# A two-layer attention and feed-forward trunk: places of the first loads, order of the context products, and four edits further on

## The chip, the cores and the metric

The kernel runs on one core of one Trainium2 chip. The metric is the time of one execution on the device in microseconds (us); the median of several runs is given. A core has a matrix engine (TensorE, PE in the profile), VectorE (DVE), ScalarE (ACT), GpSimd (POOL) and SyncE (SP), each with an instruction queue of its own, and DMA engines that move data between device memory and the on-chip memory.

## The reference

512 latent tokens and 256 context tokens of width 1024 go through two layers. Layer 0 has differential attention (4 heads) and neighbourhood attention (8 heads) side by side, layer 1 has windowed grouped-query attention with sink logits (16 query heads on 4 key heads, window 128). Every layer ends in a SwiGLU feed-forward network (FFN) of 2816 hidden columns.

```python
def rmsnorm(x, g):
    y = xf * lax.rsqrt(jnp.mean(xf * xf, axis=-1, keepdims=True) + NORM_EPS)
    return y * g
def modulate(h, shift, scale):
    return h * (1 + scale) + shift
def swiglu(h, w1, w3, w2):
    return (jax.nn.silu(h @ w1) * (h @ w3)) @ w2
# in each layer, for latent and for context tokens:
#   six modulation vectors from silu(c) @ ada_w + ada_b
#   x = x + gate_1 * mixer(modulate(rmsnorm(x, norm_g), shift_1, scale_1))
#   x = x + gate_2 * swiglu(modulate(rmsnorm(x, norm_g), shift_2, scale_2))
# after both layers: out = rmsnorm(x, final_g), latent tokens only
```

Latent queries read the latent keys and all context keys in one softmax; queries and keys of the latent tokens are rotated by position (rotary embedding). Context tokens read context tokens only, and leave after layer 0 except for their keys and values in layer 1.

## The kernel before, in words

All activations lie transposed, 128 of the 1024 features on the partitions (chunks k = 0 to 7), tokens along the columns. Each matrix product is made of three on TensorE, with both operands split into a high and a low part: high x high, high x low, low x high (`mm3`, lines 209 to 211 and their like). Weights come from device memory as `raw` tiles of 512 KB; ACT rounds the high part, DVE subtracts for the low one (`split`, lines 198 and 199; `split_by_dma`, lines 203 to 205, lets a DMA that adds do the subtraction). The class `Stream` S loads weights in the order of their use through SP's queue into a pool with three places and splits them ahead.

The order of work is set in two ways. Under `manual_schedule` an engine does its instructions in the order of the code: the start up to the first attention, for all five engines, and the second attention and the start of the second FFN for four. Elsewhere the Tile scheduler orders the instructions of each engine by itself, from the order in which the code issues them.

**Start.** `ada_load(b, k)` brings the modulation weights (b = 0, 1, eight chunks each), `w_load` four projection weights (keys, queries, two of values: `wk_raw`, `wq_raw`, `wv0_raw`, `wv1_raw`). Four modulation weights share the pool `wpool` (tag "raw") with the projection weights; TensorE reads the modulation weights at line 237. Then come the latent products (line 786), and the context part: sums of squares (`c_sq`, lines 853 to 857), their norm (lines 901 to 911), the chunks of modulated context `c_t` and `c_lo` (lines 918 to 923), and the context's products (lines 937 to 939). `rope_read` and `rope_end` (lines 891 to 896) rotate keys (`psk`) and queries (`psq`) from PSUM; `evac_pair` writes keys and queries, `swap_halves` makes `k2`, the keys with halves exchanged, through two DMAs; `v_group` is the context's values.

**First attention.** Eight units of heads, each with five steps; `run_steps` issues a step's scores (lines 1055 and 1056 for the differential heads) and softmax, then the value products of the step before, then some filling work `fillers[n]`, mostly the next unit's queries, keys and values.

**First FFN.** Products go by the `seven` products of a scheme for 2 x 2 blocks. In its last part (`down_last` at line 1583, products at lines 1563 to 1565) eight chunks m of latent and then eight of context columns get their residual on DVE (line 1557), and in the second of these loops `next_norm` makes the second layer's first norm: squares on ACT, additions on DVE and GpSimd (lines 331 to 340), a product with ones that sums over partitions (line 308), logarithm and exponential on ACT (lines 315 to 318), and `h_make` (lines 352 to 354). `apart=True` leaves three sums to be added by three products with ones.

**Second attention.** A loop over n = 0 to 33 in set order: scores (line 1748), the masked maximum on DVE (`masked`, line 1758), exponentials on ACT (`powers`, line 1765), value products four steps later; `fill(counts[n][0])` and `fill(counts[n][1])` place that many filling products before and behind the transposes, the output projection's among them (lines 1882 and 1906, residual line 1867). `to_make` queues weight roundings (lines 1828 and 1829).

**Output.** The second FFN's own `down_last` makes the last four chunks' products of the second FFN for two halves of 256 tokens, `final_norm` the norm of a half, `put_out` multiplies eight pieces on DVE and GpSimd (line 2278) and stores each (line 2279).

## Time and profile before

| What | us |
|---|---|
| Median of 3 runs | 1590.34 (1589.73 to 1591.67) |
| The profiled execution | 1589.07 |
| Its span from first to last instruction | 1587.3 |
| TensorE busy | 1544.8 |
| DVE, ACT, GpSimd busy | 1225.2, 729.7, 265.0 |

The page has busy times first, then the span in 40 slices, DMA queues, the chain of work that ended last, and groups of instructions. A row of the timeline begins with start and duration; "L308" is line 308; "f<-norm,ones" is output and inputs by the program's names; in brackets stands the idle time of the engine ahead of the row and whom it waited for. Matmuls overlap in a pipeline, so the distance of their starts is what one costs. "SPq" is SP's instruction queue. In windows, each engine has its busy us and instructions, then the granted clock of TensorE (1.00 is full), the share of the DMA engines, and GB/s.

### The profile page before, as it was taken

What the parts mean: (1) busy time and instruction counts of PE and PEld (TensorE: products, weight loads), DVE (VectorE), ACT (ScalarE), POOL (GpSimd) and SP (SyncE); (2) the same over time, 40 slices, a digit from 0 to 9 for tenths busy, and PEclk for the clock granted to TensorE, in tenths of its full rate; (3) what the DMA queues carried; (4) which work ended last, traced back from release to release, by engine and by line L of the source; (5) the groups of instructions that cost most, each with busy time, mean ns of one, the idle gap of its engine ahead of it and who ended that gap; (6) DMA issues with size and microseconds to landing.
All of it is one profiled execution on the core that took longest, in us unless ns stands there. A gap on an engine that the chain in (4) does not pass through costs nothing.

```text
span 1587.3 us, 25721 instructions
## 1 busy us (share of the span) xinstructions
PE 1544.8 (97%) x10029; PEld 1372.5 (86%) x10029; DVE 1225.2 (77%) x2090; ACT 729.7 (46%) x1242; POOL 265.0 (17%) x340
## 2 busy tenths in 40 slices
PE   8999999999999999999999999999999999999997
PEld 5898988877878999989999997877768899989896
DVE  4767798966698789879798867677666887869686
ACT  4555554445354423424424254366655533425254
POOL 1032223462010000000100002255320000000001
PEclk9999999999999999999999999999999999999999
DMA  9422254543236465475766653311013442422321
GB/s 333 127 66 74 77 176 128 185 137 93 70 120 165 115 181 159 140 210 162 215 177 166 206 135 99 92 42 41 28 54 79 134 146 80 134 67 94 121 79 54
DMA packets 68897, 196.93 MB, mean 124 GB/s; under 512 B 6836, under 2 KB 19284, under 8 KB 68776
## 3 DMA queue, kind: packets, MB, share of 16 engines
q1 hardware_dynamic: 58136, 159.95, 32.0%
q0 software_dynamic: 9632, 34.03, 9.8%
q8 instruction: 79, 1.29, 0.3%
q10 hardware_dynamic: 1008, 1.31, 0.2%
q14 instruction: 42, 0.34, 0.1%
HBM read 161.04 MB, written 4.86 MB: 105 GB/s over the span
## 4 chain that ended last, share of the span: by engine, by line
PE 57%; DMA 4%; issue 3%; DVE 3%; ACT 1%; DVEq 0%; SPq 0%; ACTq 0%; POOLq 0%; POOL 0%
PE f L1524 5%; PE f L1522 5%; PE f L1523 5%; PE f L2197 4%; PE f L2199 4%; PE f L2198 4%; PE f L1563 3%; PE f L1564 3%; PE f L1565 3%; PE lin L1859 2%; PE f L2251 2%; PE f L2250 2%; PE f L2252 2%; PE s L1748 2%; PE t L410 2%
## 5 line engine op out<-in xcount | busy, mean ns | idle before, releaser
L198 ACT ACTIVATE wh<-raw 128x1024 fp32r<-128x1024 f32 (+1 forms) x96 | 92.1, 977 | 235.6 <-DVE raw L539 94.5
L199 DVE TENSOR_TENSOR wl<-raw,wh 128x1024 fp32r<-128x1024 f32 (+1 forms) x96 | 106.9, 1119 | 40.6 <-ACT wh L198 39.1
L209 PE MATMUL lin<-hb,wh 128*128 128x512 f32 (+1 forms) x352 | 121.9, 347 | 4.1 <-ACT hb L1295 2.4
L210 PE MATMUL lin<-hb,wh 128*128 128x512 f32 (+1 forms) x352 | 119.9, 341 | 0.5 <-DVE hb L1296 0.5
L211 PE MATMUL lin<-hb,wl 128*128 128x512 f32 (+1 forms) x352 | 119.6, 340 | 0.0
L271 DVE SCALAR_TENSOR_TENSOR junk<-raw,tables 128x1024 bf16<-128x1024 f32 x80 | 98.6, 1233 | 15.6 <-DMA raw<-in_ada_wT_dram 15.1
L204 POOL DMA_DIRECT2D wl<-raw x39 | 34.1, 874 | 444.2 <-ACT wl L203 417.5
L1563 PE MATMUL f<-g,wh 128*128 128x512 f32 (+1 forms) x304 | 102.7, 339 | 0.2 <-DVE s L1552 0.2
L1564 PE MATMUL f<-g,wh 128*128 128x512 f32 (+1 forms) x304 | 102.7, 339 | 0.0
L2198 PE MATMUL f<-hb,wh 128*128 128x256 f32 x360 | 101.6, 283 | 0.0
L2197 PE MATMUL f<-hb,wh 128*128 128x256 f32 x360 | 101.4, 283 | 0.0
L2199 PE MATMUL f<-hb,wl 128*128 128x256 f32 x360 | 101.2, 283 | 0.0
L1565 PE MATMUL f<-g,wl 128*128 128x256 f32 (+1 forms) x304 | 100.7, 336 | 0.0
L1522 PE MATMUL f<-hb,wh 128*128 128x384 f32 x288 | 96.2, 334 | 0.0
L1523 PE MATMUL f<-hb,wh 128*128 128x384 f32 x288 | 96.2, 334 | 0.0
L1524 PE MATMUL f<-hb,wl 128*128 128x384 f32 x288 | 96.2, 334 | 0.0
L209 PEld LDWEIGHTS lin<-hb,wh 128*128 128x128 f32 x352 | 66.6, 189 | 15.0 <-ACT hb L1295 2.9
L210 PEld LDWEIGHTS lin<-hb,wh 128*128 128x128 f32 x352 | 66.7, 189 | 8.3 <-DVE hb L1296 0.7
L338 POOL TENSOR_TENSOR ns_a<-ns_a,ns_s 128x256 f32<-128x256 f32 (+1 forms) x8 | 8.4, 1054 | 388.3 <-ACT ns_s L334 388.3
L211 PEld LDWEIGHTS lin<-hb,wl 128*128 128x128 f32 x352 | 66.6, 189 | 7.1
L1524 PE MATMUL f<-T,wl 128*128 128x384 f32 x216 | 72.2, 335 | 0.4 <-DVE wl L199 0.4
L1522 PE MATMUL f<-T,wh 128*128 128x384 f32 x216 | 72.2, 334 | 0.0
(521 smaller groups left out, 4918.7 us busy)
## 6 DMA issues: line engine op xcount, KB each, us to landing
raw<-in_w_dram SPq DMA_DIRECT2D x132, 512.0 KB, 3.8
raw<-in_ada_wT_dram SPq DMA_DIRECT2D x80, 512.0 KB, 3.8
wl<-raw POOLq DMA_DIRECT2D x41, 512.0 KB, 6.2
raw<-in_w_ab_dram SPq DMA_DIRECT2D x24, 512.0 KB, 4.1
raw<-in_ada_w_dram SPq DMA_DIRECT2D x12, 512.0 KB, 7.7
raw<-in_w_c_dram SPq DMA_DIRECT2D x12, 512.0 KB, 4.0
nb<-in_na_bias_dram POOLq DMA_DIRECT2D x16, 256.0 KB, 3.2
raw<-in_wo_ab_dram SPq DMA_DIRECT2D x8, 512.0 KB, 3.7
```

The source lines that it names most:

```text
L209: nc.tensor.matmul(ps, wh(k), xh(k), start=k == 0, stop=False)
L210: nc.tensor.matmul(ps, wh(k), xl(k), start=False, stop=False)
L211: end = nc.tensor.matmul(ps, wl(k), xh(k), start=False, stop=k == n - 1)
L1522: nc.tensor.matmul(ps, wh(k), b[:, 0, :], start=k == 0, stop=False)
L1523: nc.tensor.matmul(ps, wh(k), b[:, 1, :], start=False, stop=False)
L1524: nc.tensor.matmul(ps, wl(k), b[:, 0, :], start=False, stop=k == 3)
L1563: nc.tensor.matmul(ps, hi, g[:, 0, cols[v]], start=first, stop=False)
L1564: nc.tensor.matmul(ps, hi, g[:, 1, cols[v]], start=False, stop=False)
L1565: nc.tensor.matmul(ps, lo, g[:, 0, cols[v]], start=False, stop=last)
L2197: nc.tensor.matmul(ps, wh(k), b[:, 0, :], start=k == 0, stop=False)
L2198: nc.tensor.matmul(ps, wh(k), b[:, 1, :], start=False, stop=False)
L2199: nc.tensor.matmul(ps, wl(k), b[:, 0, :], start=False, stop=k == 3)
```

## The change

It has five parts. (1) Four more of the modulation weights' chunks get places in buffers of the attention that are free at the start; none takes a place in `wpool` any more. (2) In the context part both `rope_read` move behind the chunks of context, one copy of values ahead of them; the context's keys and queries get other PSUM tiles; the fillers of the first step run ahead of the steps. (3) At the first FFN's end one more pair of weights is split by ACT and DVE, `next_norm` runs at m = 2 instead of 4 with one product with ones instead of three, and the activation table is loaded behind a copy. (4) In the second attention some filling products move by a step, and the last roundings are queued for the step behind the last scores. (5) The output part is written in set order, with one product with ones for the first half and two for the second, multiplications of 512 columns on DVE alone, and eight stores of 256 KB instead of sixteen of 128 KB.

```diff
@@ -559,7 +559,7 @@
...
         t = tpool[0]().rearrange("p a b n -> p (a b n)")
         hi, lo = t[:, 0:1024], t[:, 1024:2048]
-        (split if i == 1 else split_by_dma)(hi, lo, raw[0])
+        (split if i in (1, 3) else split_by_dma)(hi, lo, raw[0])
@@ -686,14 +686,17 @@
...
-            ada_at = {(1, 5): wide[1][:, NX : 3 * NX], (1, 6): sp.tile([P, 2 * NT + 128], F32, tag="q", name="xs")[:, 0:1024]}
+            ada_at = {(1, 5): wide[1][:, NX : 3 * NX]}
+            for key, tag, n in (
+                ((1, 6), "q", 2 * NT + 128), ((0, 5), "q", 2 * NT + 128), ((0, 6), "k1", 2 * NT), ((0, 7), "v", 2 * NT), ((1, 7), "k2", 2 * NT),
+            ):
+                ada_at[key] = sp.tile([P, n], F32, tag=tag, name="xs", bufs=1 if tag == "k2" else 2)[:, 0:1024]
...
-                    z = wpool if (b, k) in ((0, 5), (0, 6), (0, 7), (1, 7)) else pa
-                    t = z.tile([P, 1024], F32, tag="raw" if z is wpool else "ada", name="raw")
+                    t = pa.tile([P, 1024], F32, tag="ada", name="raw")
@@ -904,7 +907,6 @@
...
             rus = [rp.tile([P, NX], F32, tag="ru", name="ru", bufs=1), p0.tile([P, NX], F32, tag="ns_s", name="ru", bufs=2)]
-            rope_read(0, psk)
@@ -924,30 +926,35 @@
...
+            vunits[0] = sp.tile([P, 6, 256], F32, tag="v", name="v")
+
+            def v_copy(t):
+                nc.scalar.copy(vunits[0][:, 2 + 2 * t : 4 + 2 * t, :], psv[t][:, :, 0:256])
+
+            v_copy(0)
             c_t(0)
-            rope_read(1, psq)
             for k in range(KT):
                 if k < KT - 1:
                     c_t(k + 1)
                 c_lo(k)
-            pck, pcq = linp(), linp()
+            v_copy(1)
+            rope_read(0, psk)
+            rope_end(0)
+            pck, pcq = tp(), tp()
...
-            vunits[0] = sp.tile([P, 6, 256], F32, tag="v", name="v")
-            for t in range(2):
-                nc.scalar.copy(vunits[0][:, 2 + 2 * t : 4 + 2 * t, :], psv[t][:, :, 0:256])
-            rope_end(0)
             evac_pair(units[0]["k"], NC, NX, ropes[0], 1.0)
             evac_pair(units[0]["k"], 0, NC, pck[:, 0:NC], 1.0)
             swap_halves(units[0]["k2"], units[0]["k"])
+            rope_read(1, psq)
...
-            ps = tp().rearrange("p (t c) -> p t c", t=2)
+            ps = sp2((P, 2, 512))[:, :, 0:256]
             v_group(ps, 0, [tuple(wslice(z, 256) for z in w[0:2]) for w in (wv0, wv1)])
@@ -1351,7 +1358,9 @@
...
             fillers += spread(fl, len(us))
-        run_steps(steps, fillers)
+        for f in fillers[0]:
+            f()
+        run_steps(steps, [[]] + fillers[1:])
@@ -1438,7 +1447,9 @@
...
             pool = Carve([half(z, i) for z in t for i in range(2)])
-            r = rstd_of(fps(), sq_sum(xr, pool, apart=True), D, pool)
+            a, b = sq_sum(xr, pool)
+            nc.vector.tensor_add(a, a, b)
+            r = rstd_of(fps(), [a], D, pool)
             for k in range(KT):
@@ -1597,7 +1608,7 @@
...
-                if m == 4:
+                if m == 2:
                     next_norm()
@@ -1619,9 +1630,7 @@
...
-                    act = nc.scalar.activation(q, q, AF.Silu)
-                    if p == HT // 2 - 1:
-                        exp_ln_tables(act)
+                    nc.scalar.activation(q, q, AF.Silu)
                     rows(1 if p > 2 else 0, end)
@@ -1632,6 +1641,8 @@
...
                     g_made[:] = [nc.scalar.copy(g[:, 0, :], q), nc.vector.tensor_sub(g[:, 1, :], q, f32(g[:, 0, :]))]
+                    if p == HT // 2 - 1:
+                        exp_ln_tables(g_made[0])
@@ -1888,7 +1899,7 @@
...
                         keys = k2.rearrange("p a b n -> p (a b n)")
                         to_make([keys[:, 0:1024], keys[:, 1024:2048]], last)
-                        to_make()
+                        to_make(ready=last + 1)
@@ -1928,7 +1939,7 @@
...
-            (0, 4), (8, 5), (0, 4), (3, 10), (0, 2), (0, 12), (0, 4), (8, 5), (0, 4), (3, 10), (0, 2), (0, 12),
+            (0, 4), (8, 5), (0, 7), (0, 10), (0, 2), (0, 12), (0, 4), (8, 5), (0, 7), (0, 10), (0, 2), (0, 12),
@@ -2253,49 +2264,87 @@
...
-        def final_norm(i):
...
-            sq = sq_sum([x1[k][:, c] for k in range(KT)], pool, apart=i == 1)
...
-                nc.scalar.activation(ts[k], x1[k][:, c], AF.Copy, scale=fg[:, k : k + 1])
-            gains.append((ts, rstd_of(fps(), sq, D, pool)))
-
-        def put_out(i):
-            ts, r = gains[i]
-            for k in range(KT):
-                (nc.gpsimd if k in (1, 4, 7) else nc.vector).tensor_mul(ts[k], ts[k], r)
-                (nc.scalar if i and k % 2 else nc.sync).dma_start(out[:, k, halves[i]], ts[k])
-
         def down_last(js):
...
-            for ci, c in enumerate(halves):
-                for m in range(KT):
...
-                    end = to_residual(m, ps, c)
-
-                    if ci and m == 2:
-                        final_norm(0)
-            with tc.issue_after(end.ins):
-                put_out(0)
-            final_norm(1)
-            put_out(1)
+            by_hand.enter_context(tc.manual_schedule(engines={ENG.PE, ENG.DVE, ENG.Activation, ENG.Pool}))
...
+            def summed(m, c):
+                to_residual(m, ps[m, c], halves[c])
+                nc.scalar.activation(room[c][m], x1[m][:, halves[c]], AF.Square)
+                nc.scalar.activation(fo[m // 2][:, 2 * c + m % 2], x1[m][:, halves[c]], AF.Copy, scale=fg[:, m : m + 1])
+
+            def added(m, c):
+                nc.vector.tensor_add(room[c][0], room[c][0], room[c][m])
+
+            def sums(c, *squares):
+                ps[c] = fps()[:, 0:H]
+                for i, z in enumerate(squares):
+                    nc.tensor.matmul(ps[c], ones, z, start=i == 0, stop=i == len(squares) - 1)
...
+            def put_out(c, i):
+                z = fo[i][:, 2 * c : 2 * c + 2, :]
+                nc.vector.tensor_mul(z, z, small[3 * c + 1].unsqueeze(1).to_broadcast([P, 2, H]))
+                (nc.scalar if c and i % 2 else nc.sync).dma_start(out[:, 2 * i : 2 * i + 2, halves[c]], z)
+
+            for m in range(6):
+                products(m, 0, [0, 1])
+            for m in range(6):
+                products(m, 0, [2, 3])
+            for m in range(KT):
+                if m > 5:
+                    products(m, 0, range(4))
+                summed(m, 0)
+                if m > 1:
+                    added(m - 1, 0)
+            added(7, 0)
+            for m in range(KT):
+                products(m, 1, range(4))
+                if m == 1:
+                    sums(0, room[0][0])
+                if m == 2:
+                    root(0)
+                summed(m, 1)
+                if m > 2:
+                    added(m - 1, 1)
+                if m == 2:
+                    root_end(0)
+                    added(1, 1)
+                if 2 < m < 7:
+                    put_out(0, m - 3)
+            sums(1, room[1][0], room[1][7])
+            root(1)
+            root_end(1)
+            for i in range(KT // 2):
+                put_out(1, i)
+            by_hand.close()
```

What stands on SP's queue from the first modulation weight to the first loads of the stream, before:

```order
L698 DMA raw<-in_ada_w_dram 128x2x512 x6
L703 DMA raw<-in_w_ab_dram 128x1024 x3
L712 DMA crow_dram<-tables 2x1024
L698 DMA raw<-in_ada_w_dram 128x2x512 x5
L698 DMA xs<-in_ada_w_dram 128x2x512 x2
L698 DMA raw<-in_ada_w_dram 128x2x512
L703 DMA raw<-in_w_ab_dram 128x1024
L825 DMA res<-in_ctxT_dram 128x512 x4
L827 DMA tables<-in_rope_dram 128x512 x2
L144 DMA raw<-in_w_ab_dram 128x1024 x5
```

And now, on the same queue (`xs` are the attention's buffers, `in_ctxT` is the context):

```order
L701 DMA raw<-in_ada_w_dram 128x2x512 x3
L701 DMA xs<-in_ada_w_dram 128x2x512 x3
L706 DMA raw<-in_w_ab_dram 128x1024 x3
L715 DMA crow_dram<-tables 2x1024
L701 DMA raw<-in_ada_w_dram 128x2x512 x5
L701 DMA xs<-in_ada_w_dram 128x2x512 x3
L706 DMA raw<-in_w_ab_dram 128x1024
L144 DMA raw<-in_w_ab_dram 128x1024
L828 DMA res<-in_ctxT_dram 128x512 x4
L830 DMA tables<-in_rope_dram 128x512 x2
L144 DMA raw<-in_w_ab_dram 128x1024 x4
```

The loads stand in the same order as before, but more of them go to `xs`, and one weight of the stream (L144) has moved ahead of the context's four loads.

DVE in the context part, from the norm's last steps to the first chunks, before (`ns_t` and `ns_y` belong to the norm, `hb` are the chunks, `ru` and `rbuf` the rotary reads):

```order
L905 TENSOR_SCALAR ns_s<-t 128x256
L891 STREAM_SHUFFLE ru<-lin 128x512
L892 TENSOR_TENSOR rbuf<-lin,tables 128x512
L910 SCALAR_TENSOR_TENSOR ns_t<-ns_t,ns_s 128x256
L911 SCALAR_TENSOR_TENSOR ns_y<-ns_t,ns_y 128x256
L918 SCALAR_TENSOR_TENSOR ns_h<-res,amod_112,ns_y 128x256
L891 STREAM_SHUFFLE ru<-lin 128x512
L892 TENSOR_TENSOR rbuf<-lin,tables 128x512
L918 SCALAR_TENSOR_TENSOR ns_h<-res,amod_112,ns_y 128x256
L923 SCALAR_TENSOR_TENSOR hb_114<-ns_h,mod_110,hb_114 128x256
```

And now, from the last two chunks to the queries' read, on the same engine:

```order
L925 SCALAR_TENSOR_TENSOR hb_120<-ns_h,mod_110,hb_120 128x256
L925 SCALAR_TENSOR_TENSOR hb_121<-ns_h,mod_110,hb_121 128x256
L894 STREAM_SHUFFLE ru<-lin 128x512
L895 TENSOR_TENSOR rbuf<-lin,tables 128x512
L898 TENSOR_TENSOR ru<-ru,tables 128x512
L161 TENSOR_TENSOR wl<-raw,wh 128x1024
L899 TENSOR_TENSOR rbuf<-rbuf,ru 128x512
L161 TENSOR_TENSOR wl<-raw,wh 128x1024
L371 SCALAR_TENSOR_TENSOR k_526<-rbuf,k_526 64x512 x2
L371 SCALAR_TENSOR_TENSOR k_526<-t,k_526 64x256 x2
L894 STREAM_SHUFFLE ru<-lin 128x512
L895 TENSOR_TENSOR rbuf<-lin,tables 128x512
```

The keys' read has moved from ahead of the norm's last two steps to behind the last chunk, and the queries' read from between the first two chunks to behind the keys.

DVE at the end of the program, from the last residual on, before:

```order
L2239 SCALAR_TENSOR_TENSOR res<-f,mod_111,res 128x256
L340 TENSOR_TENSOR ns_a<-ns_a,ns_s 128x256
L2239 SCALAR_TENSOR_TENSOR res<-f,mod_111,res 128x256
L2278 TENSOR_TENSOR fo<-fo,ns_y 128x256 x5
L316 TENSOR_SCALAR ns_v<-f 128x256
L319 SCALAR_TENSOR_TENSOR ns_t<-ns_t,ns_v 128x256
L320 SCALAR_TENSOR_TENSOR ns_y<-ns_t,ns_y 128x256
L2278 TENSOR_TENSOR fo<-fo,ns_y 128x256 x5
```

And now:

```order
L2250 SCALAR_TENSOR_TENSOR res<-f,mod_111,res 128x256
L2293 TENSOR_TENSOR sum<-sum 128x256
L2314 TENSOR_TENSOR fo<-fo,s_15454 128x512
L2250 SCALAR_TENSOR_TENSOR res<-f,mod_111,res 128x256
L2293 TENSOR_TENSOR sum<-sum 128x256
L2303 TENSOR_SCALAR s_15454<-f 128x256
L2309 SCALAR_TENSOR_TENSOR s<-s,s_15454 128x256
L2310 SCALAR_TENSOR_TENSOR s<-s 128x256
L2314 TENSOR_TENSOR fo<-fo,s_15454 128x512 x4
```

The first half's multiplications (5 of its 8 were on DVE, behind the last residual) stand among the second half's residuals, each twice as wide, and all four of the second half are on DVE.

More of the change, by code (lines that the diff above doesn't have):

```diff
@@ L2254, in down @@
                     to_residual(4 * i + m, ps[m], slice(0, NX))
-        fo, gains = [], []
-        def norm_tiles(i):
-            a = (spool[0], "sum", 2) if i else (fp, "s", 2)
-            return PoolMap(ns_a0=a, ns_a1=a, ns_s=(fp, "q", 2), ns_v=(fp, "s", 2), ns_y=a, ns_t=(fp, "s4", 1))
-        def final_norm(i):
-            c = halves[i]
-            pool = norm_tiles(i)
-            sq = sq_sum([x1[k][:, c] for k in range(KT)], pool, apart=i == 1)
-            ts = []
-            for k in range(KT):
-                if i == 0 and k % 2 == 0:
-                    fo.append(fp.tile([P, 4, H], F32, tag=f"ts{k // 2}", name="fo"))
-                ts.append(fo[k // 2][:, 2 * i + k % 2])
-                nc.scalar.activation(ts[k], x1[k][:, c], AF.Copy, scale=fg[:, k : k + 1])
-            gains.append((ts, rstd_of(fps(), sq, D, pool)))
@@ L2275, in put_out @@
-        def put_out(i):
-            ts, r = gains[i]
-            for k in range(KT):
-                (nc.gpsimd if k in (1, 4, 7) else nc.vector).tensor_mul(ts[k], ts[k], r)
-                (nc.scalar if i and k % 2 else nc.sync).dma_start(out[:, k, halves[i]], ts[k])
         def down_last(js):
             w = [S.next(4, 3) for _ in js]
-            for ci, c in enumerate(halves):
-                for m in range(KT):
-                    ps = fps()[:, 0:H]
-                    mc = slice(m * P, (m + 1) * P)
-                    mm3(
-                        ps, lambda k: w[k][0][:, mc], lambda k: w[k][1][:, mc],
-                        lambda k: gt[js[k]][:, 0, c], lambda k: gt[js[k]][:, 1, c], n=len(js),
-                    )
-                    end = to_residual(m, ps, c)
-                    if ci and m == 2:
-                        final_norm(0)
-            with tc.issue_after(end.ins):
-                put_out(0)
-            final_norm(1)
-            put_out(1)
+            by_hand.enter_context(tc.manual_schedule(engines={ENG.PE, ENG.DVE, ENG.Activation, ENG.Pool}))
@@ new lines, in down_last @@
+            ps, sq, root_of = {}, {}, {}
+            room = [[fp.tile([P, 4 * H], F32, tag="q", name="q", bufs=2) for _ in range(2)], [spool[0].tile([P, 1024], F32, tag="sum", name="sum") for _ in range(2)]]
+            room = [[z[:, H * i : H * i + H] for z in y for i in range(4)] for y in room]
+            small = fp.tile([P, 4 * H], F32, tag="s4", name="s4", bufs=1)
+            small = [small[:, H * i : H * i + H] for i in range(4)] + [fp.tile([P, H], F32, tag="s", name="s", bufs=2) for _ in range(2)]
@@ new lines, in down_last, with products @@
+            fo = [fp.tile([P, 4, H], F32, tag=f"ts{k}", name="fo") for k in range(KT // 2)]
+            def products(m, c, ks):
+                if ks[0] == 0:
+                    ps[m, c] = fps()[:, 0:H]
+                for k in ks:
+                    hi, lo = (z[:, m * P : (m + 1) * P] for z in w[k])
+                    g = gt[js[k]]
+                    nc.tensor.matmul(ps[m, c], hi, g[:, 0, halves[c]], start=k == 0, stop=False)
+                    nc.tensor.matmul(ps[m, c], hi, g[:, 1, halves[c]], start=False, stop=False)
+                    nc.tensor.matmul(ps[m, c], lo, g[:, 0, halves[c]], start=False, stop=k == len(js) - 1)
@@ new lines, in root, with root_end @@
+            def root(c):
+                v, y, t = small[3 * c : 3 * c + 3]
+                nc.scalar.activation(t, ps[c], AF.Ln, bias=epst, scale=1.0 / D)
+                nc.vector.tensor_scalar(v, ps[c], 1.0 / D, EPS, op0=ALU.mult, op1=ALU.add)
+                nc.scalar.activation(y, t, AF.Exp, scale=-0.5)
+                nc.scalar.activation(t, y, AF.Square)
+            def root_end(c):
+                v, y, t = small[3 * c : 3 * c + 3]
+                nc.vector.scalar_tensor_tensor(t, t, -0.5, v, op0=ALU.mult, op1=ALU.mult)
+                nc.vector.scalar_tensor_tensor(y, t, 1.5, y, op0=ALU.add, op1=ALU.mult)
```

## The prediction

> **What bounds the kernel now.** I read the engines' busy times, then TensorE's waits, then each place of the change on the timeline, with the engine that TensorE waits for there.
>
> ```profile
> span 1587.3 us, 25721 instructions
> PE 1544.8 (97%) x10029; PEld 1372.5 (86%) x10029; DVE 1225.2 (77%) x2090; ACT 729.7 (46%) x1242; POOL 265.0 (17%) x340
> ```
>
> TensorE (PE) is busy for 1544.8 of 1587.3 us, so it is the bound: what can be won are its 42.5 idle us, matmuls that go away, and stretches at a lower clock. Who was waited for (total us, times, longest):
>
> ```profile
> PE s L1056 <- DMA k<-k: 2.6, 2, 1.7
> PE t L237 <- DMA raw<-in_ada_w_dram: 2.6, 2, 1.9
> PE s L1748 <- ACT p L1765: 2.1, 2, 1.4
> PE f L1565 <- DMA T<-raw: 1.6, 1, 1.6
> PE t L209 <- ACT hb L353: 1.5, 1, 1.5
> PE t L1193 <- DVE ns_v L316: 1.2, 1, 1.2
> PE lin L1882 <- DVE res L1867: 1.0, 2, 0.8
> ```
>
> The reader is to see that no wait is longer than 1.9 us, and that most edits stand before one of them (L1193 excepted): several gains of 1 to 3 us, no large one.
>
> **The change part by part.** The sums are against the profiled execution (1589.07 us, of it 1587.3 span); the median of the runs, 1590.34, lies 1.27 above it, and that is added at the end.
>
> *First loads.* Some of the first weights on SyncE's queue (SP) wait for a buffer that TensorE still reads. The rows are one of SP's waits, then busy times, granted clock and DMA share of three stretches, then a row of TensorE and two of ScalarE (ACT):
>
> ```profile
> SPq L703 <- PE t L237: 2.3, 3, 1.0
> ...
> 18.00:20.00 2.00, 2.00 (x22) 0.94 (x21) 1.82 (x3) 0.03 (x1) 0.00 (x0) 1.00 1.04 380
> 20.00:28.00 8.00, 6.19 (x46) 3.81 (x45) 6.11 (x14) 4.50 (x6) 0.00 (x0) 1.00 0.88 292
> 30.00:34.00 4.00, 4.00 (x19) 2.15 (x16) 4.00 (x7) 0.48 (x1) 0.00 (x0) 0.57 1.03 391
> ...
> 29.56 0.64 PE L237 MATMUL t<-raw,craw 128*32 128x256 f32 x8 [1.87 <-DMA raw<-in_ada_w_dram]
> ...
> 41.73 0.71 ACT L856 ACTIVATE ns_s<-res 128x256 f32<-128x256 f32 x2
> 44.12 1.52 ACT L759 ACTIVATE hb<-xs,mod,amod 128x512 fp32r<-128x512 f32 x2 [1.68 <-DVE amod L259]
> ```
>
> While those loads wait, the DMA engines run at 0.88 instead of 1.04 for 8 us: (1.04 - 0.88) x 8 / 1.04 = 1.2 us of transfer lost. With places of their own the modulation weights no longer share buffers with the projection weights, and the 1.87 us wait at 29.56 loses 1.2 at least. The clock of 0.57 right behind it costs 0.43 x 4 = 1.7 us; without the wait it may stay full. At most 1.87 + 1.7 = 3.6 us, and 0.4 more from an earlier wait on the same queue. Next late is L759, the modulated x of chunk 4. It waits in order on ACT behind L856, the squares of the context, which end at 42.44; the context loads do not come earlier, because one more 512 KB weight load now stands ahead of them on SP. So L759 starts at 42.4 instead of 44.1, and 1.7 is what that chain gives. I take 2.2, between 1.7 and 3.6; bounds 0.5 (the queue is refilled elsewhere) and 4.
>
> *Context products.* VectorE (DVE) rows from the context's norm to its last product, then TensorE at the first scores:
>
> ```profile
> 55.95 0.74 DVE L891 STREAM_SHUFFLE ru<-lin 128x512 f32<-128x512 f32 x1
> 57.18 0.41 DVE L910 SCALAR_TENSOR_TENSOR ns_t<-ns_t,ns_s 128x256 f32<-128x256 f32 x1
> 58.49 0.74 DVE L891 STREAM_SHUFFLE ru<-lin 128x512 f32<-128x512 f32 x1
> 59.72 0.47 DVE L918 SCALAR_TENSOR_TENSOR ns_h<-res,amod,ns_y 128x256 f32<-128x256 f32 x1
> ...
> 56.05 0.42 ACT L909 ACTIVATE ns_t<-ns_y 128x256 f32<-128x256 f32 x1
> ...
> 67.45 0.28 PE L431 MATMUL t<-wh,hb 128*128 128x256 f32 x1
> 78.75 0.28 PE L1055 MATMUL s<-k,q 128*128 128x256 f32 x1
> 80.76 0.36 PE L1056 MATMUL s<-k,q 128*128 128x256 f32 x1 [1.74 <-DMA k<-k]
> ```
>
> The two rotary reads stand inside the chain: the first holds L910 from 56.5 (its input from ACT is ready at 56.05 + 0.42) to 57.18, 0.7 us; the second the next L918 from 58.49 to 59.72, 1.2 us. Without them the eight chunks start 1.9 us earlier at an unchanged pace, and TensorE, which ends their products at 67.45, is paced by them. From there to 78.75 it runs 48 matmuls of 256 columns and 24 of 512, as much as 96 of 256: 11.3 / 96 = 0.12 us each. The change puts 24 more of 256 columns, 2.9 us, ahead of the first scores, beside the swap of the keys, for which L1056 now waits 1.74. The first read, 1.2, now stands ahead of the keys: the swap lands at 80.76 - 1.9 + 1.2 = 80.1. TensorE is there at 78.75 - 1.9 + 2.9 = 79.75, so some 0.4 of the wait is left: 1.9 + 1.74 - 0.4 = 3.2. The second read stands ahead of the queries, which may end at 80.3; I take 3.0; bounds 1 (queries or swap a further 2 us late) and 3.7 (no wait left).
>
> *First attention.* The first step's filling matmuls run ahead of it, and the scheduler then gives another order for most of the first attention:
>
> ```profile
> 80.00:348.00 268.00, 263.79 (x1805) 233.78 (x1807) 214.30 (x375) 141.25 (x311) 95.57 (x107) 1.00 0.39 119
> 348.00:460.00 112.00, 104.48 (x695) 85.04 (x693) 81.99 (x132) 52.27 (x108) 24.80 (x36) 1.00 0.34 104
> ```
>
> TensorE's idle time there is 4.2 us, 0.8 of it the wait above. So at most 3.4 can be won. A loss has its nearest row in L1193's wait of 1.2, the one of eight head norms there that TensorE waits for; four more of them are 4.8. I take 0, as nothing tells the sign, and bounds of -5 and +3.4.
>
> *End of the first FFN.* The last weights were split through a DMA (ACT, GpSimd's queue, a transfer); now ACT copies and DVE subtracts. Then comes the norm. The last row has clock and DMA share:
>
> ```profile
> 947.31 1.06 ACT L203 ACTIVATE T<-raw 128x1024 fp32r<-128x1024 f32 x1 [5.21 <-DMA raw<-in_w_dram]
> ...
> 950.72 1.76 DVE L1634 TENSOR_TENSOR g<-q,g 128x1536 fp32r<-128x1536 f32 x1 [7.13 <-ACT g L1634]
> 966.57 0.68 DVE L340 TENSOR_TENSOR norm<-norm 128x512 f32<-128x512 f32 x1
> 979.88 1.41 DVE L352 SCALAR_TENSOR_TENSOR norm<-res,amod,csr 128x512 f32<-128x512 f32 x2
> ...
> 955.80 0.50 PE L1565 MATMUL f<-g,T 128*128 128x512 f32 x1 [1.60 <-DMA T<-raw]
> ...
> 972.89 2.73 PE L308 MATMUL f<-norm,ones 128*128 128x512 f32 x6
> ...
> 982.00:986.00 4.00, 3.79 (x14) 3.15 (x13) 3.96 (x7) 2.37 (x5) 3.36 (x8) 0.57 0.76 277
> ```
>
> ACT has copied by 948.4, and DVE is idle for 7.13 us before 950.72, which hides a subtraction of some 1.2: it ends at 949.6, and TensorE comes at 954.2. Gain 1.6 (bounds 1.3 and 1.7; without DVE's idle time it would still have 4 us). The six L308 matmuls are three products, 2.2 us by the distance to the next row; one is left, so 1.45 go. Two more additions (0.68 each) and a residual stand on DVE behind 967.25 and end by 969.1; the product stands 10 matmuls (1.2 us) earlier, at 971.7, and hides them. So L352 starts 2.65 earlier, TensorE comes 1.45 earlier, and its 1.5 us wait for L353 shrinks by 1.2. Some of it goes to residuals that now fall among L352 to L354: I take 2.2 for both; bounds 1, where L352 to L354 on DVE, 1.4 a pair, pace TensorE anyway, and 4, with the clock of 0.57 gone too (1.7).
>
> *Second attention.* Residuals are made before the masked maximum, and the last roundings a step later:
>
> ```profile
> 1185.53 0.62 ACT L1828 CAST wh<-raw 128x512 fp32r<-128x512 f32 x1 [4.98 <-DMA raw<-in_w_dram]
> ...
> 1184.06 0.14 DVE L1758 DVE_READ_ACCUMULATOR2_ANT mx<- 128x1 f32 x1
> ```
>
> ACT stands 4.98 us before a rounding whose weight is not there. The first exponential behind it could start at 1184.2, when its maximum is read, and starts at 1186.1. Moved, this saves 1.2 to 1.5 of the 2.1 that TensorE waits for L1765; the residual's wait (L1867, 1.0) mostly goes. I take 2.0; bounds 0.7 and 3.2. The rounded weight is for the FFN behind this attention, so a step later is covered.
>
> *Output.* Rows of the tail, with the size and landing time of two kinds of DMA:
>
> ```profile
> 1573.85 1.00 DVE L340 TENSOR_TENSOR ns_a<-ns_a,ns_s 128x256 f32<-128x256 f32 x1 [0.55 <-ACT ns_s L334]
> 1578.95 3.35 DVE L2278 TENSOR_TENSOR fo<-fo,ns_y 128x256 f32<-128x256 f32 x5
> ...
> 1575.88 0.64 PE L308 MATMUL f<-ns_s,ones 128*128 128x256 f32 x2
> ...
> nb<-in_na_bias_dram POOLq DMA_DIRECT2D x16, 256.0 KB, 3.2
> ...
> out_dram<-fo SPq DMA_DIRECT2D x12, 128.0 KB, 1.8
> ```
>
> One ones-product less in the middle and one at the end (0.5 each), the last addition at 0.4 instead of 1.0, and four multiplications of 512 columns, 2.7 at L340's 0.68, for 3.35: 0.5 + 0.5 + 0.6 + 0.65 = 2.25. The last transfer is twice as large: 0 to 1.4 later by the two landing times; 0.8 taken. Gain 1.4; bounds 0.3 and 2.5.
>
> Sum: 2.2 + 3.0 + 0 + 1.6 + 2.2 + 2.0 + 1.4 = 12.4; 1589.07 - 12.4 = 1576.7, against the median 1577.9.
>
> **The rivals.** *The gains do not add up.* Each removed wait lets the next late thing show: L759 behind the context's squares, queries instead of keys, DVE's pairs at the FFN's end. For it speaks that DVE works 3.96 of the 4 us behind 982. Then the low bounds hold, 0.5 + 1 + 1.3 + 1 + 0.7 + 0.3 = 4.8, or up to half the sum: about 1584.5.
>
> *The clock falls without the waits.* The two stretches at 0.57 follow waits of 1.87 and 1.5, while the one of 1.74 left it at 1.00 (the row from 80), so the wait need not be the cause. If they stay or come elsewhere, the gains of waits are kept and each new stretch costs 1.7: one more gives 1579.6, both gone beyond my sum about 1576. [...]
>
> *Slower: the first attention loses its cover.* It has 40 softmax steps (8 units of 5), and their filling is placed anew. If each left TensorE waiting 0.5, 40 x 0.5 = 20, less the 3.4 there now: 16.6 more, 1594.5. From 0.48 a step on (12.4 + 3.2 lost) the kernel is slower than 1593.5. Against it: in the 268 us DVE, the next busiest, works 214, and only the first step loses its own filling.
>
> *It does nothing.* If the early loads, scores and roundings are bound by the transfers themselves (DMA share 1.03 from 30 to 34), little but the two products is left: about 1588.
>
> **How the numbers follow.** My forecast has 0.60, the sum in part 0.24, the other clock 0.05 (within the forecast's range), the lost cover 0.05, nothing 0.06. About 0.2%, 3.2 us, is what a measurement of this kernel tells from no change. Faster than 1587.1 are the first three, 0.89; the same 0.07; slower 0.04, a part of the lost cover staying within. The widths of the bounds, mostly independent (5 for the first attention, under 2 for each other part), give 12.4 ± 5.5, 1572.4 to 1583.4; with the partial sum the range is 1572 to 1585.5, and the predicted time 1578.
>
> **What would show it.** Right: no L237 wait over 0.7 and clock 1.00 at 30 to 34; the last context product at about 63 and first scores at 78 (the start's gain included); one L308 product at the first FFN's end and no wait on T<-raw; the L1765 and L1867 waits under 0.6; the end 11 to 12 us behind the last product of the last FFN instead of 13. Wrong: TensorE idle over 6 us between 80 and 348, or a late query where the key swap was.

## The result, and the profile after

The changed kernel takes 1577.61 us in the median (1573.41 to 1578.88, 4 runs), the kernel before 1590.03 (1589.07 to 1591.67, 4 runs). The ratio is 0.9916, with a 95% interval of 0.9896 to 0.9936: 12.4 us less, where 12.4 were forecast. How that sum came together is another matter, and the rest of this document is about it. Two further measurements of the same kernel gave 0.9908 (0.9882 to 0.9935) and 0.9922 (0.9901 to 0.9943).

The span and the busy times on the page of the changed kernel:

```profile
span 1575.6 us, 25696 instructions
PE 1540.2 (98%) x10021; PEld 1369.0 (87%) x10021; DVE 1228.7 (78%) x2097; ACT 728.8 (46%) x1241; POOL 257.1 (16%) x329
```

TensorE is busy for 4.6 us less and idle for 35.4 instead of 42.5. Of the 11.7 us of span, 7 are waits, the rest is products with ones that went away and one stretch at half clock less (ahead of the last 10 us one here, from 12.93, and two before, from 30.16 and 982.48, each 3.41 us at 0.50). Its waits (total us, times, longest):

```profile
PE f L1535 <- DVE wl L199: 2.2, 2, 1.7
PE lin L209 <- DVE k L379: 2.0, 2, 1.4
...
PE s L401 <- ACT p L1183: 1.6, 3, 0.8
...
PE s L1063 <- DMA k<-k: 1.3, 2, 0.8
PE t L1200 <- DVE ns_v L316: 1.1, 1, 1.1
...
PE f L2298 <- DVE sum L2293: 0.9, 1, 0.9
...
PE t L209 <- ACT hb L353: 0.6, 1, 0.6
```

The reader is to see three things. The waits that the edits stood before are gone or small: none is left in this profile for the modulation weights, the last weights' DMA, the exponentials and the residual of the second attention; the swapped keys have 0.8 (longest), the norm 0.6. Two rows are new or much larger: L209 waits for keys (L379) inside the first attention, and L1535 for a split weight in the first FFN, which no edit touches. And the last sum on VectorE (L2293) holds TensorE for 0.9 at the end, as L340 did for 0.7.

### The profile page after: what moved, and what is told of

Read it like the earlier page. It is cut to its first block, busy times and chain, and to the rows that moved or that the text cites. A ratio compares the mean times of both kernels' runs of the same rounds, so it can differ in the third digit from the quotient of the medians.

```text
span 1575.6 us, 25696 instructions
## 1 busy us (share of the span) xinstructions
PE 1540.2 (98%) x10021; PEld 1369.0 (87%) x10021; DVE 1228.7 (78%) x2097; ACT 728.8 (46%) x1241; POOL 257.1 (16%) x329
## 4 chain that ended last, share of the span: by engine, by line
PE 51%; DVE 6%; issue 5%; DMA 4%; ACT 1%; POOL 0%; SPq 0%; DVEq 0%; POOLq 0%; ACTq 0%
PE f L1535 4%; PE f L1534 4%; PE f L1533 4%; PE f L2208 4%; PE f L2209 4%; PE f L2210 4%; PE f L1574 2%; PE f L1575 2%; PE f L1576 2%; PE lin L1870 2%; PE s L1759 2%; PE f L2262 2%; PE f L2263 2%; PE f L2261 2%; PE t L410 2%
## 5 line engine op out<-in xcount | busy, mean ns | idle before, releaser
L199 DVE TENSOR_TENSOR wl<-raw,wh 128x1024 fp32r<-128x1024 f32 (+1 forms) x96 | 106.9, 1120 | 39.7 <-ACT wh L198 39.1
L209 PE MATMUL lin<-hb,wh 128*128 128x512 f32 (+1 forms) x352 | 121.7, 347 | 5.5 <-DVE k L379 2.0
L1535 PE MATMUL f<-hb,wl 128*128 128x384 f32 x288 | 96.3, 334 | 0.0
L209 PEld LDWEIGHTS lin<-hb,wh 128*128 128x128 f32 x352 | 66.6, 189 | 16.9 <-issue 2.7
L1535 PE MATMUL f<-T,wl 128*128 128x384 f32 x216 | 72.3, 336 | 2.2 <-DVE wl L199 2.2
L1534 PE MATMUL f<-T,wh 128*128 128x384 f32 x216 | 72.2, 334 | 0.0
L1533 PE MATMUL f<-T,wh 128*128 128x384 f32 x216 | 72.2, 334 | 0.0
```

Source lines behind the costliest of these rows:

```text
L209: nc.tensor.matmul(ps, wh(k), xh(k), start=k == 0, stop=False)
L1533: nc.tensor.matmul(ps, wh(k), b[:, 0, :], start=k == 0, stop=False)
L1534: nc.tensor.matmul(ps, wh(k), b[:, 1, :], start=False, stop=False)
L1535: nc.tensor.matmul(ps, wl(k), b[:, 0, :], start=False, stop=k == 3)
```

## The experiments

Twelve more runs followed, three of them of the two kernels unchanged. Each leaves a profile, which makes fourteen with the first two, so every stretch of the program was seen several times with its old code and several times with its new. That turned out to be what decides here, because one execution differs from the next by more than any single edit is worth: runs of the kernel before lay between 1584.3 and 1597.1, and on one and the same chip between 1586.2 and 1597.1. The times:

| Kernel | median us (runs) | ratio to the kernel before, interval |
|---|---|---|
| first loads only | 1589.43 (12) | 0.9988 (0.9973 to 1.0003) |
| context part only | 1589.95 (12) | 0.9980 (0.9968 to 0.9993) |
| first FFN's end only | 1589.34 (12) | 0.9979 (0.9963 to 0.9995) |
| second attention only | 1587.51 (12) | 0.9965 (0.9949 to 0.9981) |
| kernel before, again | 1589.36 (1) | |
| changed kernel, again | 1574.88 (4) | 0.9908 (0.9882 to 0.9935) |
| changed, values in the other PSUM tile | 1576.59 (4) | 0.9912 (0.9880 to 0.9943) |
| changed, two weights more split by engines | 1574.20 (4) | 0.9903 (0.9877 to 0.9929) |
| changed kernel, third time | 1577.09 (4) | 0.9922 (0.9901 to 0.9943) |
| changed, with both of these edits | 1576.99 (4) | 0.9919 (0.9896 to 0.9942) |
| last roundings only | 1587.47 (1) | |
| changed, one product of the output on GpSimd | 1575.23 (1) | |

The next table holds the stages. Each is the time between the starts of two TensorE instructions in the trace, named by where they stand in the first profile of before (the first stage begins with the span, the last ends with it). Mean and range stand over the profiles in which the stage has its old code, then its new code, with their number. This takes it that an edit acts in its own stage alone.

| Stage | old code | new code | gained | forecast |
|---|---|---|---|---|
| start to the context's sum product (54.0) | 52.4, 51.6 to 54.0 (6) | 50.9, 50.3 to 51.4 (8) | 1.5 | 2.2 |
| from there to 352 | 298.6, 297.6 to 300.0 (6) | 297.5, 297.0 to 298.3 (6) | 1.1 | 3.0 |
| 352 to 950, no edit in it | 597.1 to 603.5 (12) | | | |
| 950 to 957, last weights | 5.8, 5.1 to 7.0 (6) | 5.1 (8) | 0.7 | 1.6 |
| 957 to 1000, norm | 42.8, 41.9 to 43.0 (6) | 39.7 (8) | 3.1 | 2.2 |
| 1100 to 1250, second attention | 150.7, 149.5 to 152.8 (5) | 145.7, 145.4 to 146.3 (8) | 5.0 | 2.0 |
| 1549 to the end | 38.2 to 38.3 (7) | 35.9 (6) | 2.4 | 1.4 |

The gains add to 13.8 us; 1000 to 1100 gives 0.3 back. That is what the three ratios of the changed kernel show (12.4, 13.6 and 13.2 us). A single stage without an edit, 352 to 950, differs by 6.4 us between executions, while 1250 to 1549 takes 299.0 in all fourteen.

### The first loads alone

```diff
+                ((1, 6), "q", 2 * NT + 128), ((0, 5), "q", 2 * NT + 128), ((0, 6), "k1", 2 * NT), ((0, 7), "v", 2 * NT), ((1, 7), "k2", 2 * NT),
...
-                    z = wpool if (b, k) in ((0, 5), (0, 6), (0, 7), (1, 7)) else pa
```

> Only the places of the first loads are changed. If the removed buffer waits are the gain: no wait of TensorE for the modulation weights over 0.7 us, the clock 1.00 from 30 to 34, the context's sum product 2.2 to 2.7 us earlier than at 54.0, the same lead at the first scores and behind the first attention, and a time 2.2 us lower (0.14%). If the lead is given back (keys' swap or weight transfers set the pace later): the lead at 54 is the same, but under 0.8 us of it is left by 460, and the time is within 0.05%. If the clock does not hang on the wait: a stretch at half clock stays and the lead at 54 is only 1 us.

The context's sum product came at 51.2 us, 2.85 earlier than in the first profile, and 2.2 of that are left at 352, but the time is only 0.12% lower, not told from none. The kernel before, profiled again, explains the difference:

> The kernel before, unchanged, profiled once more. If the stages in which the other unchanged copies of the code differed are chance of an execution: the context's sum product comes at 52 to 52.5 us instead of 54.0 and the clock is 1.00 from 30 to 34; the first FFN loses 0 to 5 us against the first profile between 640 and 740; the wait for the last weights near 954 is anything from 0 to 1.6. If the first profile shows what the kernel does: 54.0, the same two stretches at half clock, 1.6.

It came at 51.6. The rows are windows of this second profile of before; the last three columns are the granted clock, the DMA share and GB/s:

```profile
26.00:30.00 4.00, 2.91 (x19) 1.27 (x23) 3.33 (x5) 4.00 (x6) 0.00 (x0) 1.00 1.00 368
30.00:34.00 4.00, 4.00 (x28) 2.29 (x26) 4.00 (x7) 0.36 (x1) 0.00 (x0) 1.00 1.05 398
```

The same windows of the changed kernel:

```profile
26.00:30.00 4.00, 4.00 (x30) 1.91 (x28) 3.19 (x6) 4.00 (x7) 0.00 (x0) 1.00 1.05 388
30.00:34.00 4.00, 4.00 (x32) 2.29 (x25) 4.00 (x6) 1.28 (x2) 0.00 (x0) 1.00 1.05 387
```

TensorE works 2.91 of the 4 us before 30 in the one and all 4 in the other. Its waits for the modulation weights come to 1.3 to 2.6 us in the six profiles of the old code and to 0 to 1.2 in the eight of the new, 1.8 and 0.7 on the mean: this is the edit, 1.1 us. What it ends is the wait near 29 (0.6 to 1.9 in all six, none in the eight); the one near 22 stays in seven of the eight. The stretch at 0.57 from 30 to 34 stood in the first profile alone, and its 1.7 us were an accident of that execution. One more profile of the old code and two of the new have a half-clock stretch elsewhere in the first 30 us (the changed kernel's first from 12.93 to 16.34, at 0.50). The four old and six new profiles without any give 52.03 - 50.75 = 1.3, all of them 1.5.

### The context part alone, and the first attention

```diff
+            v_copy(1)
+            rope_read(0, psk)
...
-            ps = tp().rearrange("p (t c) -> p t c", t=2)
+            ps = sp2((P, 2, 512))[:, :, 0:256]
```

> Only the context part is changed (order of the rotary reads, PSUM tiles of keys, queries and values). If the reads held the chain: the last context product at 65.4 to 65.8 instead of 67.3, and the 24 matmuls that stand ahead of the first scores end 3.0 to 3.4 us earlier than before. If the new order of the first attention costs something of itself: TensorE's idle time from there to 348 is 1 to 2 us higher than the 3.4 of before, so that 1.2 to 2.2 us are left by 350. If that loss in the changed kernel was chance: the full 3 us are left by 350.

From the context's sum product to its last product the changed code takes 11.7 us, the old one 13.3, in every profile: 1.6, where 1.9 were forecast. The 24 products and the first scores end 27.9 us behind the sum product (27.4 to 28.5 in six profiles) where the old code takes 31.1 (30.1 to 32.0): 3.2 us, as forecast. But at 352 only 1.1 is left (0.7 in this run). Three waits of TensorE in the changed kernel, on its timeline:

```profile
216.72 0.50 PE L209 MATMUL lin<-hb,wh 128*128 128x512 f32 x1 [0.63 <-DVE k L379]
...
246.09 0.50 PE L209 MATMUL lin<-hb,wh 128*128 128x512 f32 x1 [1.39 <-DVE k L379]
...
344.48 0.98 PE L401 MATMUL s<-k,q 64*128 64x256 f32 x12 [0.72 <-ACT p L1183]
```

At these three places the kernel before waits 0.0, 0.44 and 0.0. Those of 1.4 and 0.7 stand in all six profiles with the new order, the one of 0.6 in five, so the order makes them and not the execution. They come to some 2.3 us more. Two waits that both orders have are shorter on the mean with the new one: for swapped keys near 157, 0.6 instead of 1.1, and for `pt` near 302, 0.6 instead of 1.3. So TensorE's idle time from the block of first scores to 352 rises by 1.4 us, from 4.3 to 5.7, of the 2.1 that the stage gave back; a half-clock stretch in one profile makes 0.3 of the mean, and for the rest, longer busy time, no row was found. What made the order new? The kernel with the context part alone leaves out the two lines that run the first step's filling ahead, and its TensorE, VectorE and ScalarE go through the first attention in the same order as in the changed kernel, so these lines change no order. The PSUM tile of the context's values does it:

```diff
-            ps = sp2((P, 2, 512))[:, :, 0:256]
+            ps = tp().rearrange("p (t c) -> p t c", t=2)
```

> The changed kernel with the context's values in a PSUM tile of the kind of before, so that the order of the first attention is again that of before from the third step on. If that tile is what reorders it and costs: from the block of first scores to 352 it takes 267 us instead of 269 to 270; but the first scores stand ahead of the 24 matmuls again and wait 2 to 3 us for the swapped keys: both cancel, time within 1 us of the changed kernel. If the longer way through the first attention is chance: 269 here too, and 2 us slower.

Without that tile TensorE's order is that of before again from about 116 us on, and the three waits are gone: 267.4 us from the block of first scores to 352, and 268.4 in a second kernel without it (with both edits, below), against 268.9 to 270.8 with it and 266.9 to 268.1 in the old code. But the first scores did not stand ahead of the 24 products again, as I had expected: the latent products now come ahead of the values, and wait 1.4 us for split weights (0.78 for ScalarE, 0.66 for VectorE, near 64), so the block takes 29.5. From the sum product to 352 it is 296.9, within the 297.0 to 298.3 of the other tile but for 0.1, and the time shows no difference.

### The wait in the first FFN

In nine of the twelve profiles without the next edit TensorE waits 1.2 to 4.0 us in this FFN ahead of its last weights, mostly for a split weight near 733. In the third profile of the changed kernel, between 640 and 760:

```profile
PE f L1535 <- DVE wl L199: 1.7, 1, 1.7
PE f L1533 <- DVE res L1568: 1.3, 1, 1.3
```

> The changed kernel, unchanged. The stages that hang on the order alone repeat within 0.1 us (context's sum to last context product 11.8, norm at the first FFN's end), and those that hang on when a transfer lands do not (the wait of 1.7 near 733, the first 16 us). Time 1576 to 1579.

> The changed kernel, unchanged, beside the next one on the same chip. 1574 to 1578; the first attention's three waits near 216, 245 and 344 us (0.6, 1.4 and 0.7) stand again, as they hang on the order; the wait near 733 may or may not.

The second profile of the changed kernel has no such wait, the first and third have, with the same order; it seems to hang on when a load lands, as VectorE's longest wait for one near 690 is 4.9 to 7.4 us in the nine profiles and 4.4 to 5.5 in the three without. The three other waits stand again, but for the one near 216 in the third profile. My reading was that the load's place is held by a weight that is split through a DMA, so the next kernel splits two of these by ScalarE and VectorE:

```diff
-                made = plain_parts if sg == supers0[1] and i else dma_parts
+                made = plain_parts if sg == supers0[1] and i or sg == supers0[2] and i > 1 else dma_parts
```

> The changed kernel with two weights of the first FFN's second block more split by ScalarE and VectorE instead of through a DMA. If the detour holds the place of a load that comes too late: VectorE's wait for it near 690 (5.5 us and 7.0) falls under 4, TensorE has no wait over 0.6 between 680 and 740 (1.7 in the changed kernel, up to 3.3 in the others), and the time is 1 to 3 us lower. If VectorE (two subtractions of 1.2 more) or the transfer itself is the bound: the wait near 735 stays 1.5 or more and the time is the same or higher.

> The changed kernel with both edits: the context's values in the other kind of PSUM tile, and two weights more split by ScalarE and VectorE. If the order of the first attention is what gave back the start's gain: none of the waits near 216 (0.6) and 344 (0.7) and 0.4 instead of 1.4 near 245, but 1.4 of wait ahead of the values, so 1 to 1.5 us less from the context's sum to 352; no wait over 0.6 near 733. Time 1 to 2 us below the changed kernel. If both only shift chance: the same time.

Neither kernel has a wait over 0.4 there. VectorE still waits 4.6 and 4.4 us for the load near 690 (4.8 in the second profile of the changed kernel, 7.0 in its first), so its wait did not fall under 4 as expected. Two profiles without the wait, where three of twelve lack it anyway, do not settle it, and the times of 1574.20 and 1576.99 lie within the changed kernel's runs (1572.7 to 1578.9). The kernel with both edits did not take less from the sum product to 352 either (297.9): the three waits of the first attention are gone there too, but its waits for swapped keys near 158 and for `pt` near 300 are 2.2 and 1.4. No version was found that beats the changed kernel.

### The end of the first FFN alone

```diff
-        (split if i == 1 else split_by_dma)(hi, lo, raw[0])
+        (split if i in (1, 3) else split_by_dma)(hi, lo, raw[0])
...
-                if m == 4:
+                if m == 2:
                     next_norm()
```

> Only the end of the first FFN is changed (last weights split by ScalarE and VectorE, norm at m = 2 with one product with ones, table load moved). If waits and products add up as forecast: 1.6 us earlier at the last weights' products, 3 us earlier at the first products of the next norm, with or without the clock. If the clock falls because of the wait of 1.5 us: it stays 1.00 behind the shorter wait, and 4 to 5 us are won by 1000; if it falls by chance of its own: a stretch near 0.57 stays in the 10 us behind, and 3 are won. Time 3 to 4 us lower (0.2 to 0.25%).

TensorE's rows of this kernel (start, duration, wait in brackets):

```profile
973.93 1.02 PE L308 MATMUL f<-norm,ones 128*128 128x512 f32 x2
...
981.02 0.50 PE L209 MATMUL t<-hb,wh 128*128 128x512 f32 x1 [0.56 <-ACT hb L353]
982.31 0.50 PE L210 MATMUL t<-hb,wh 128*128 128x512 f32 x1 [0.56 <-DVE hb L354]
```

One product with ones is left and the wait of 1.5 has become two of 0.56. From 957 to 1000 every profile of the new code takes 39.7 us and no half clock follows; five of six of the old code take 43.0 with a stretch at half clock, one 41.9 without: 2.2 us by the edit itself and 1.1 by the clock, which fell behind the old wait in five of six (0.50 from 982.48 to 985.89 in the first profile, behind the wait of 1.50; 0.63 from 982 to 986 in the one with the second attention alone). From 950 to 957 the new code always takes 5.1, but so did three of six profiles of the old. Only in the first profile is the DMA the whole wait (1.6); in two others TensorE waits 0.4 and 0.5 for VectorE's `g` (L1634), then at most 0.3 for the DMA. So the wait of 1.6 was the longest seen, and the edit is worth 0.7 on the mean. Against the first profile this run won 5.2 us by 1000, where 4 to 5 were expected; on the mean of all profiles it is 3.8.

### The second attention

```diff
-            (0, 4), (8, 5), (0, 4), (3, 10), (0, 2), (0, 12), (0, 4), (8, 5), (0, 4), (3, 10), (0, 2), (0, 12),
+            (0, 4), (8, 5), (0, 7), (0, 10), (0, 2), (0, 12), (0, 4), (8, 5), (0, 7), (0, 10), (0, 2), (0, 12),
...
-                        to_make()
+                        to_make(ready=last + 1)
```

> Only the second attention is changed (six filling products moved, last roundings queued one step later). If the residuals and the early roundings were the waits: TensorE waits under 0.3 us for the residual (1.0 before) and under 0.6 for the exponentials at 1185 to 1188 (2.1 before), 0.8 to 1.0 us from the first and 1.2 to 1.5 or more from the second, 2.0 to 3.0 us together. If another late input takes their place: under 1 us, with a wait of TensorE over 0.6 for something else between 1130 and 1230.

> Only the last roundings of the second attention are queued a step later. If the rounding in front of the exponentials is the whole wait at 1184 to 1190: 2.5 us earlier there, as in the kernel with the whole part, and nothing at 1134 and 1166 (1.0 and 0.4 belong to the filling products). If the filling products share in it: under 2.

With the whole part TensorE's waits from 1124 to 1196 are one row:

```profile
PE t L410 <- ACT pt L1801: 0.5, 1, 0.5
```

With the last roundings alone (1125 to 1200) they are:

```profile
PE lin L1882 <- DVE res L1867: 1.0, 2, 0.8
PE t L410 <- ACT pt L1801: 0.5, 1, 0.5
PE s L1748 <- ACT p L1765: 0.4, 1, 0.4
```

So the roundings end 1.7 of the 2.1 us for the exponentials, and the filling products the residual's 1.0 and the last 0.4. By the distance of TensorE's starts the whole part won 1.0 at 1134, 0.4 at 1166 and 2.5 at 1184 to 1190, against the first profile; the roundings alone 1.7 at the last place, so the products share in it, and the expectation of 2.5 was too high. The 3.9 in all are more than the 2.0 to 3.0 expected, and 0.8 more than the idle time of the four waits (3.1). In the first profile of before:

```profile
1180.62 1.15 PE L1748 MATMUL s<-gk,gq 64*128 64x258 f32 x12
...
1186.99 0.38 PE L1748 MATMUL s<-gk,gq 64*128 64x258 f32 x1 [1.41 <-ACT p L1765]
1188.04 0.97 PE L1748 MATMUL s<-gk,gq 64*128 64x258 f32 x11 [0.67 <-ACT p L1765]
```

Twelve scores that overlap take 1.15 us, one that a wait cuts off takes 0.38 alone: so a wait costs some 0.2 us here beyond its bracket, an estimate from these rows (0.38 + 0.97 - 1.15). In two other profiles the old code lost 1.2 and 2.8 us more: there the waits near 1185 were followed by half clock (0.50 from 1187.4 to 1190.8 in the kernel with the first FFN's end alone).

### The output

This part was not run alone. The six profiles with its code as it is in the changed kernel have 35.9 us from 1549 on, whatever the other edits, and one kernel moves a multiplication back to GpSimd:

```diff
-                nc.vector.tensor_mul(z, z, small[3 * c + 1].unsqueeze(1).to_broadcast([P, 2, H]))
+                if c and i == 1:
+                    for j in range(2):
+                        nc.gpsimd.tensor_mul(z[:, j], z[:, j], small[3 * c + 1])
+                else:
+                    nc.vector.tensor_mul(z, z, small[3 * c + 1].unsqueeze(1).to_broadcast([P, 2, H]))
```

> The changed kernel with one of the last four multiplications of 512 columns given to GpSimd as two of 256. If VectorE and GpSimd slow each other: the three on VectorE take over 0.75 us each instead of 0.62, those on GpSimd 0.7 to 1 each, and the end comes within 0.2 us of the changed kernel's or later (8.8 us behind TensorE's last matmul). If they do not: VectorE is done 0.6 us earlier, and the end 0.3 to 0.6 earlier.

VectorE's last multiplications in the changed kernel, on its timeline:

```profile
1569.18 2.50 DVE L2314 TENSOR_TENSOR fo<-fo,s 128x512 f32<-128x512 f32 x4
```

and in this one, three on VectorE and two half as wide on GpSimd:

```profile
1565.54 2.95 DVE L2318 TENSOR_TENSOR fo<-fo,s 128x512 f32<-128x512 f32 x3
...
1565.73 2.21 POOL L2316 TENSOR_TENSOR fo<-fo,s 128x256 f32<-128x256 f32 x2 [349.15 <-issue]
```

Three take longer than four did: beside GpSimd's two they took 0.98 us each instead of 0.62, and those on GpSimd 1.1 each. The end came 10.3 us behind TensorE's last matmul instead of 8.8. The kernel before shows longer multiplications beside GpSimd too. Its five multiplications on VectorE take 1.90 us for the first half, 0.38 each, when GpSimd's three are almost done, and 3.35 for the second half, 0.67 each, beside GpSimd's three:

```profile
1575.17 1.90 DVE L2278 TENSOR_TENSOR fo<-fo,ns_y 128x256 f32<-128x256 f32 x5
...
1578.95 3.35 DVE L2278 TENSOR_TENSOR fo<-fo,ns_y 128x256 f32<-128x256 f32 x5
...
1573.15 2.29 POOL L2278 TENSOR_TENSOR fo<-fo,ns_y 128x256 f32<-128x256 f32 x3
1578.99 2.69 POOL L2278 TENSOR_TENSOR fo<-fo,ns_y 128x256 f32<-128x256 f32 x3 [3.55 <-DVE ns_y L320]
```

## Why the prediction was right or wrong, point by point

**The sum** was right, 12.4 us for 12.4 to 13.6 measured, by errors that cancel: it was too high for the first loads by 0.7, the context with the first attention by 1.9 and the last weights by 0.9, and too low for the norm by 0.9, the second attention by 3.0 and the output by 1.0. Two parts came out outside their own bounds: the last weights with 0.7 (1.3 to 1.7) and the second attention with 5.0 (0.7 to 3.2). That the sum met the time so closely is luck.

**First loads**: the mechanism was right, the term mis-sized. "The clock of 0.57 right behind it costs 0.43 x 4 = 1.7 us; without the wait it may stay full" went into the 2.2 in part, and only one of six profiles of the old code has that stretch: 1.5 measured, 1.3 without any half clock. L759 came as forecast: in the changed kernel it starts at 42.48, right behind the context's squares. But TensorE waits at most 0.24 us for ScalarE between 31 and 51 in any profile, so the 1.7 of that chain was no limit of TensorE's. The squares themselves now wait 0.8 to 1.3 us for the context's loads in all eight profiles of the new code and in none of the six of the old.

**Context products**: right, product by product. The last one came at 63.05, forecast about 63; the first scores at 77.3 with a wait of 0.8 for the swapped keys, forecast 78 and 0.4; the block gained 3.2, forecast 3.0.

**First attention**: here a step failed. "The first step's filling matmuls run ahead of it, and the scheduler then gives another order" names the wrong cause, as those lines change no order and the PSUM tile of the values does; and "I take 0, as nothing tells the sign" missed three waits of 2.3 us; the stage takes back 2.1 of the 3.2, of which 1.4 is idle time. It lay within the bounds of -5 and +3.4, and the rival of gains that do not add up held at this place alone.

**First FFN's end**: both mechanisms right, both sizes off. The split by engines ended the DMA's wait, but the 1.6 of the first profile was the longest of six, and the mean was 0.7. The two products with ones and the shorter wait brought 2.2 as forecast, and the clock, kept for the upper bound, stayed full in all eight profiles and was worth 1.1 us where it had fallen, not 1.7: 3.1 in all on the mean.

**Second attention**: "I take 2.0" was mis-sized. I left 0.6 or more of the wait for the exponentials standing and priced the waits by their idle time; all of it went, 3.1 us of idle time and 3.9 by the starts at the three places. The stage gained 4.3 against the first profile and 5.0 on the mean, as two other profiles of the old code had half clock there; some 0.4 was not traced to a wait.

**Output**: "0.8 taken" for larger stores was too much, as the last ones landed 2.2 to 2.5 us behind their issue where the smaller ones took 1.8. That is at most 0.4 of the 1.0; the four multiplications, 2.50 instead of 2.7, are 0.2 more, and the rest was not taken apart.

**The other rivals**: the first attention did not lose its cover of 0.5 in each step; TensorE's idle time there rose by 1.4 us on the mean in place of the 16.6 of that rival. That the change does nothing fell with the interval. The rival of the clock was half right: it fell elsewhere too, but in none of the five stretches of the last section without waits: in the 3.41 us ahead of each TensorE worked 1.45 to 1.70.

## What to carry to other kernels

A wait read off one profile is one sample: before a sum is made of such waits, take two or three profiles of the same program and keep those that repeat (the context's chain: 13.3 us in all six) apart from those that hang on a transfer's landing (0 to 1.6 us at one place, 0 to 4.0 within the first FFN). Price a wait by the distance of the starts around it, as it can cost more than its idle time (3.9 us for 3.1 in the second attention). Where a scheduler decides, the kind of PSUM tile of one product can reorder a whole stage behind it, while lines that are moved may change no order at all: compare the orders before naming a cause. Two engines that each take a share of a last elementwise pass can be slower than one (2.95 us for three multiplications on VectorE beside GpSimd's share, 2.50 for all four on VectorE alone).

## What the runs showed of the hardware

Five stretches of 3.41 us at a granted clock of 0.50 are read off here, each behind a stretch of the same length in which TensorE was idle for about half. In the kernel with the first loads alone:

```profile
359.95:363.36 3.41, 1.60 (x17) 1.19 (x16) 1.48 (x4) 1.58 (x4) 1.84 (x4) 1.00 0.76 228
363.36:366.77 3.41, 3.17 (x16) 2.05 (x18) 3.19 (x6) 3.15 (x6) 0.76 (x1) 0.50 0.33 111
```

and in the one with the first FFN's end alone:

```profile
1184.00:1187.40 3.40, 1.45 (x8) 0.78 (x6) 1.25 (x4) 2.45 (x7) 0.59 (x1) 1.00 0.61 187
1187.40:1190.80 3.40, 3.34 (x19) 3.12 (x20) 2.44 (x7) 1.61 (x5) 1.57 (x2) 0.50 0.00 0
```

TensorE worked 1.60 and 1.45 us of the first stretch, was idle for 1.81 and 1.95, and the clock of the second is 0.50. In the first profile of before the clock is 0.50 from 30.16 to 33.57, behind 3.41 us with 1.54 of work, and from 982.48 to 985.89, behind 1.70; in the first of the changed kernel from 12.93 to 16.34, behind 1.65. Elsewhere these two profiles show 1.00, up to the end (0.50 from 1579.81 and from 1569.41 on, with no matmul left). But as little work did not always cost the clock. The stretch of the first profile with the wait of 1.74 for the swapped keys had 1.67 of 3.41 us of work, less than the 1.70 ahead of 982.48, and the next stayed at 1.00:

```profile
77.95:81.36 3.41, 1.67 (x9) 1.23 (x8) 3.26 (x8) 0.51 (x2) 1.33 (x2) 1.00 0.63 149
81.36:84.77 3.41, 3.41 (x28) 3.28 (x28) 2.04 (x4) 1.87 (x4) 3.17 (x5) 1.00 0.45 139
```

So some 1.7 us of idle time in 3.41 was followed by half clock in one place, where up to another 1.7 us can be lost (half of 3.41, an estimate), and by full clock in another; what decides between them was not shown.
